# Dealing the blocks of U ahead unevenly over the three tiles of gates

## The chip, the cores and the metric

The kernel runs on one core of one Trainium2 chip. The metric is the device time of one launch in microseconds (us). Five engines run their own instruction queues in order: TensorE (PE, with PEld for its weight loads), VectorE (DVE), ScalarE (ACT), GpSimd (POOL) and SyncE (SP, which issues most DMAs). A plan made when the kernel is built fixes the order of every queue; on the chip an instruction waits only for the semaphores that it names.

## The reference

One decoder layer over 512 tokens of width 1024, all in float32. First comes token mixing (two attention groups, an output projection, a residual). Then comes a feed-forward part that looks experts up by product keys, and the change lies there:

```python
def chunk(hc):                                   # per token
    s1, s2 = scores of 8 heads against two sets of 128 keys
    v1, i1 = lax.top_k(s1, 16); v2, i2 = lax.top_k(s2, 16)
    best_s, best_pos = lax.top_k(16 x 16 sums, 16)
    expert = i1 * 128 + i2 at best_pos           # 8 x 16 of 16384 experts
    g = softmax(best_s)
    act = gelu(hc . u[expert])
    return sum over (head, k) of g * act * v[expert]
```

A last RMS norm follows.

## The kernel before

The 512 tokens are four tiles of 128. For tiles 0 to 2 the feed-forward part is dense: all 16384 experts are computed as 128 blocks of 128 experts, and a matrix of gates, nonzero at the chosen experts only, picks them. For tile 3 the 128 chosen rows of U and V per token are gathered by indirect DMA instead (`gather_ops`, L916).

**A block of U** (`u_block`, L874) loads 512 KB (SP), splits it into a high part (`uhi`, ScalarE) and a low part (`ulo`, VectorE, or GpSimd for every fourth block below 56), runs 24 matmuls (`p_u`, TensorE) and a Gelu (`a`, ScalarE). `raw`, `hi` and `lo` have two buffers each. The loads and splits have high priority in the plan (`UPRI`).

**The gates.** `route` (L713) scores the keys and takes the top 16 on VectorE, `choose` (L749) finds the experts, `spread` (L792) turns the result by TensorE transposes (`tp_s`) and makes three tables on VectorE (`o16`, `o8`). Then, for each tile, eight groups of sixteen tokens follow, each in two halves: `hot` (L816) makes one-hot factors on VectorE (`oh0` to `oh2`, two buffers each), `gates` (L831) multiplies them on TensorE (`p_g`, 16 matmuls a half), ScalarE copies the result out of PSUM (`st`, two copies a half), and after both halves SP stores 1 MB (`g_d`).

**The gathers of tile 3.** `gu` is a row of U gathered by GpSimd and multiplied on VectorE (L921). Its buffers are those of the four transposed queries `qT`, four of them, which come free as `route` has read them.

**U ahead.** The blocks of V need the gates of all three tiles, the blocks of U don't. So 56 blocks of U (`NAHEAD`) are dealt out among the work on the gates by `u_ahead`: `U0` of them ahead of the first tile's gates (L939, L941), then `GPAT[tg]` after each group of sixteen tokens (L959), then what is left (L962). The first 16 results (`NSPILL`) go out to DRAM (`a_d`). The planner then moves instructions by priority and buffers, so that what a queue holds is not quite the order of the code.

**The V part** (from L1042) has, for each of 128 blocks: a load of V (`v`), its split (`vhi`, `vlo`), a load of the spilled activations (`ar`) for the first 16, a load of the gates for every eighth (`gt`), the weights (`w`, `wh`, `wl`) and 18 matmuls (`acc`). From block 16 on a block of U follows each block of V.

Of the kernel before, what the change touches and what calls it, by code (L numbers as in the profile page):

```python
# [47 lines left out]
NGP = (0, 0, 0, 0, 1, 2, 3, 3)  # L48
M5 = 2
RLAG = 1  # L50
U0 = (4, 2)
GPAT = (2, 2, 2, 2, 2, 2, 2, 2)
WAN = (1, 2)
XAT = (0, 1)
UPRI = 1000
# [19 lines left out]
def hybrid_layer(ctx: ExitStack, tc, x, pos, wada, wada_n, cols, w_small, w_in_a, w_in_b, wuk, wuv,  # L75
# [15 lines left out]
    def one(name, tag="tp"):  # L91
        return ps.tile([P, 512], F32, tag=tag, name=name, bufs=BANKS[tag])
# [699 lines left out]
    def spread(j, sel3):  # L792

        i1 = rp.tile([P, 3, P], I32, tag="i1", name=f"i1_{j}")
        nc.vector.tensor_copy(i1[:, 0], sel3[:, 0])
        nc.vector.tensor_scalar(i1[:, 1], i1[:, 0], 4, None, op0=ALU.arith_shift_right)
        nc.vector.tensor_scalar(i1[:, 2], i1[:, 0], 15, None, op0=ALU.bitwise_and)
        f1 = rp.tile([P, 2, P], F32, tag="f1", name=f"f1_{j}")
        nc.vector.tensor_copy(f1, i1[:, 1:3])
        tp = one(f"tp_s{j}")  # L800
        for i, src in enumerate((f1[:, 0], f1[:, 1], sel3[:, 1], sel3[:, 2])):
            nc.tensor.transpose(tp[:, i * P:(i + 1) * P], src, ident)
        tt = rp.tile([P, 5, P], F16, tag="tt", name=f"tt{j}")
        nc.scalar.activation(tt[:, 0:3], tp[:, 0:3 * P].rearrange("p (i t) -> p i t", t=P), AF.Copy)
        nc.scalar.activation(tt[:, 3], tp[:, 3 * P:4 * P], AF.Copy, scale=GSCALE)
        nc.vector.scalar_tensor_tensor(tt[:, 4], tp[:, 3 * P:4 * P], GSCALE, tt[:, 3], op0=ALU.mult, op1=ALU.subtract)
        pairs = lambda i, n: tt[:, i].rearrange("p (q e) -> p q e", e=2).unsqueeze(2).to_broadcast([P, P // 2, n, 2])
        o16 = rq.tile([P, P // 2, 16, 2], F16, tag="o16", name=f"o16_{j}")
        o8 = [rq.tile([P, P // 2, 8, 2], F16, tag=f"o8_{i}", name=f"o8_{i}_{j}") for i in range(2)]
        nc.vector.tensor_tensor(o16, pairs(1, 16), iota8.unsqueeze(1).to_broadcast([P, P // 2, 16, 2]), op=ALU.is_equal)  # L810
        nc.vector.tensor_tensor(o8[1], pairs(0, 8), iota8[:, 0:8].unsqueeze(1).to_broadcast([P, P // 2, 8, 2]), op=ALU.is_equal)
        nc.vector.tensor_tensor(o8[0], o8[1], pairs(3, 8), op=ALU.mult)
        nc.vector.tensor_tensor(o8[1], o8[1], pairs(4, 8), op=ALU.mult)
        return tt, o16, o8

    def hot(j, tg, half, tt, o16, o8):  # L816

        sh, sh5 = [P, 4, NK, 2], [P, 4, 8, 16, 2]
        t0 = tg * 16 + half * 8
        qs = slice(t0 // 2, t0 // 2 + 4)  # L820
        oh = [rq.tile([P, 4, NK, 2], F16, tag=f"oh{i}", name=f"oh{i}_{j}_{tg}_{half}", bufs=2) for i in range(3)]
        nc.vector.tensor_tensor(oh[2], tt[:, 2, t0:t0 + 8].rearrange("p (q e) -> p q e", e=2).unsqueeze(2).to_broadcast(sh),
                                iota2.unsqueeze(1).to_broadcast(sh), op=ALU.is_equal)
        for i in range(2):
            nc.vector.tensor_tensor(oh[i].rearrange("p q (a b) e -> p q a b e", b=16), o8[i][:, qs].unsqueeze(3).to_broadcast(sh5),  # L825
                                    o16[:, qs].unsqueeze(2).to_broadcast(sh5), op=ALU.mult)
        return oh
# [46 lines left out]
    def u_block(b, psum):  # L874
        with tc.high_priority(offset=UPRI):
            raw = up.tile([P, KC, P], F32, tag="raw", name=f"u{b}", bufs=2)
            nc.sync.dma_start(raw.rearrange("p k e -> p (k e)"), ut[b])
            hi = up.tile([P, KC, P], F32R, tag="hi", name=f"uhi{b}", bufs=2)
            lo = up.tile([P, KC, P], F32R, tag="lo", name=f"ulo{b}", bufs=2)
            nc.scalar.activation(hi, raw, AF.Copy)  # L880
            (nc.gpsimd if b in UPOOL else nc.vector).tensor_tensor(lo, raw, hi.bitcast(F32), op=ALU.subtract)  # L881
        o = psum(f"p_u{b}")[:, :DT]
        for k in range(KC):
            mm3(o, hi[:, k], lo[:, k], h2[0][:, k], h2[1][:, k], k == 0, k == KC - 1)
        spilt = b < NSPILL
        a = up.tile([P, DT], F32, tag="as" if spilt else "a", name=f"a{b}", bufs=2 if spilt else NACT)
        nc.scalar.activation(a, o, AF.Gelu)  # L887
        if spilt:
            nc.sync.dma_start(a_d[b], a)
            a = a_d[b]  # L890
        acts.append(a)
# [3 lines left out]
    def u_ahead(n):  # L895
        for _ in range(n):
            if nu[0] < NAHEAD:
                u_block(nu[0], lambda n: one(n, ("pj", "po", "ix")[nu[0] % 3]))
                nu[0] += 1

    def chosen(j):
        sel3 = choose(j, *lists[j])
        if j == NT - 1:
            nc.vector.scalar_tensor_tensor(e0, sel3[:, 0], float(NK), sel3[:, 1], op0=ALU.mult, op1=ALU.add)
            nc.vector.tensor_copy(g0, sel3[:, 2])
        return sel3
# [31 lines left out]
    route(1, 0, *lists[0])  # L938
    u_ahead(U0[0])  # L939
    sel3 = chosen(0)  # L940
    u_ahead(U0[1])  # L941
    waiting = []

    def gates_all():
        while waiting:
            gates(*waiting.pop(0))

    for j, coming in ((0, (3, 1)), (1, (2,)), (2, ())):
        tt = spread(j, sel3)
        for tg in range(P // 16):  # L950
            for half in range(2):
                waiting.append((j, tg, half, hot(j, tg, half, *tt)))
            gates_all()
            for i, jn in enumerate(coming):
                if tg == WHEN[i][0]:
                    route(1, jn, *lists[jn])
                if tg == WHEN[i][1]:
                    sel3 = chosen(jn)
            u_ahead(GPAT[tg])  # L959
            for _ in range(NGP[tg] if j == ND - 1 else 0):  # L960
                next(gen)
    u_ahead(NAHEAD)  # L962
# [167 lines left out]
```

## Time and profile before

| what | us |
|---|---|
| median of 3 runs | 1616.62 (1614.98 to 1617.26) |
| the profiled execution | 1614.71 |
| its span | 1612.8 |

The profile's span is cut into stretches by hand, at marks on TensorE: the first matmul of U (441.3), the first matmul of the gates of tile 0 (497.5), of tile 1 (603.5), of tile 2 (688.5), the last of tile 2 (758.7), and the first matmul of V (781.2). After that the V part runs to the end of the span.

### The profile page before, as it was taken

How to read it: one execution, taken by the hardware profiler on the slowest of the kernel's cores; microseconds unless marked ns; L12 is line 12 of the kernel's file. 1: busy time of each engine (PE TensorE's matmuls, PEld its weight loads, DVE VectorE, ACT ScalarE, POOL GpSimd, SP SyncE). 2: the span in 40 equal slices, each digit the busy share in tenths (PEclk: the TensorE clock that was granted, in tenths of full speed). 3: DMA queues.
4: the chain of work that ended last, by engine and by line, in shares of the span. 5: the costliest groups of instructions: out<-in, count | busy, mean ns of one | idle time of the engine just before them, and what ended most of it. 6: DMA issues, size and time to landing. Idle time of an engine off the chain costs nothing.

```text
span 1612.8 us, 22930 instructions
## 1 busy us (share of the span) xinstructions
PE 1509.9 (94%) x8136; PEld 1328.4 (82%) x8138; DVE 1287.0 (80%) x2659; ACT 713.4 (44%) x1142; POOL 529.3 (33%) x403
## 2 busy tenths in 40 slices
PE   5887998999899989989999999999999999999997
PEld 5755776877688888889889999999999999988886
DVE  7899964856999999983569887878888788768886
ACT  4654544544245675765333333333333333323333
POOL 2333022212110220221016454554555445534420
PEclk7998997999999999999999999999999999999999
DMA  8643012514044654575979998999989999879974
GB/s 340 217 148 131 1 40 78 171 54 133 14 139 161 222 207 169 215 266 190 314 259 342 364 344 327 354 311 350 336 310 356 311 349 345 311 271 326 317 257 157
DMA packets 152899, 383.39 MB, mean 238 GB/s; under 512 B 11712, under 2 KB 66384, under 8 KB 149456
## 3 DMA queue, kind: packets, MB, share of 16 engines
q1 hardware_dynamic: 114912, 246.45, 45.0%
q0 software_dynamic: 36864, 134.23, 22.0%
q8 instruction: 64, 1.05, 0.3%
q10 hardware_dynamic: 1008, 1.24, 0.2%
q14 instruction: 51, 0.42, 0.1%
HBM read 349.36 MB, written 32.51 MB: 237 GB/s over the span
## 4 chain that ended last, share of the span: by engine, by line
PE 52%; DVE 3%; DMA 2%; issue 1%; ACT 1%; SPq 0%; POOL 0%; DVEq 0%; POOLq 0%; ACTq 0%
PE acc L1014 30%; PE p_u L149 7%; PE p_u L148 7%; PE p_u L147 7%; DMA ar<-a_d 1%; DVE gu L921 1%; DMA u<-in_ut_dram 1%; PE p_g L841 0%; DVE oh L825 0%; ACT st L844 0%; DVE vlo L993 0%; DMA x1b<-x_d 0%; DVE ulo L881 0%; DMA v<-in_pv_dram 0%; DVE o L1035 0%
## 5 line engine op out<-in xcount | busy, mean ns | idle before, releaser
L147 PE MATMUL p_u<-h,uhi 128*128 128x384 f32 x1024 | 349.7, 342 | 1.4 <-ACT a L887 1.4
L149 PE MATMUL p_u<-h,ulo 128*128 128x384 f32 x1024 | 349.2, 341 | 0.6 <-DVE ulo L881 0.5
L148 PE MATMUL p_u<-h,uhi 128*128 128x384 f32 x1024 | 348.8, 341 | 0.0
L913 POOL DMA_INDIRECT gu<-in_un_dram,e x128 | 191.5, 1496 | 296.6 <-DVE gu L921 201.5
L880 ACT ACTIVATE uhi<-u 128x1024 fp32r<-128x1024 f32 x128 | 135.8, 1062 | 292.2 <-PE p_u L148 250.9
L913 POOL DMA_INDIRECT gv<-in_pv_dram,e x128 | 191.2, 1493 | 208.6 <-DVE acc L932 163.2
L1014 PE MATMUL acc<-vhi,wh 128*128 128x512 f32 x768 | 237.1, 389 | 1.2 <-ACT wh L1006 1.2
L1014 PE MATMUL acc<-vlo,wh 128*128 128x512 f32 x768 | 237.4, 389 | 0.3 <-DVE vlo L993 0.3
L1014 PE MATMUL acc<-vhi,wl 128*128 128x512 f32 x768 | 237.1, 389 | 0.0
L1006 ACT ACTIVATE wh<-w 128x384 fp32r<-128x384 f32 x128 | 67.3, 526 | 303.4 <-issue 182.1
L147 PEld LDWEIGHTS p_u<-h,uhi 128*128 128x128 f32 x1024 | 195.0, 190 | 4.6 <-ACT a L887 1.7
L148 PEld LDWEIGHTS p_u<-h,uhi 128*128 128x128 f32 x1024 | 195.5, 191 | 2.9
L149 PEld LDWEIGHTS p_u<-h,ulo 128*128 128x128 f32 x1024 | 195.4, 191 | 1.6 <-DVE ulo L881 0.8
L1007 DVE TENSOR_TENSOR wl<-w,wh 128x384 fp32r<-128x384 f32 x128 | 71.5, 558 | 138.1 <-ACT wh L1006 137.8
L881 DVE TENSOR_TENSOR ulo<-u,uhi 128x1024 fp32r<-128x1024 f32 x114 | 139.0, 1219 | 51.9 <-ACT uhi L880 35.1
L1014 PEld LDWEIGHTS acc<-vlo,wh 128*128 128x128 f32 x768 | 144.0, 188 | 30.8 <-DVE vlo L993 1.0
L1014 PEld LDWEIGHTS acc<-vhi,wl 128*128 128x128 f32 x768 | 144.1, 188 | 30.2
L932 DVE SCALAR_TENSOR_TENSOR acc<-gv,w,acc 128x1024 f32<-128x1024 f32 x127 | 162.5, 1279 | 4.6 <-DMA gv<-in_pv_dram,e 4.6
L921 DVE SCALAR_TENSOR_TENSOR gu<-gu,h2n 128x1024 f32<-128x1024 f32 x128 | 158.8, 1255 | 8.0 <-DMA gu<-in_un_dram,e 7.7
L1014 PEld LDWEIGHTS acc<-vhi,wh 128*128 128x128 f32 x768 | 143.2, 188 | 26.0 <-ACT wh L1006 1.5
L993 DVE TENSOR_TENSOR vlo<-v,vhi 128x1024 fp32r<-128x1024 f32 x128 | 156.2, 1220 | 3.8 <-ACT vhi L992 3.8
L992 ACT ACTIVATE vhi<-v 128x1024 fp32r<-128x1024 f32 x128 | 135.6, 1059 | 9.2 <-PE acc L1014 4.3
(354 smaller groups left out, 2361.2 us busy)
## 6 DMA issues: line engine op xcount, KB each, us to landing
u<-in_ut_dram SPq DMA_DIRECT2D x128, 512.0 KB, 5.2
v<-in_pv_dram SPq DMA_DIRECT2D x128, 512.0 KB, 5.0
g_d<-st SPq DMA_DIRECT2D x24, 1024.0 KB, 4.8
gt<-g_d SPq DMA_DIRECT2D x48, 512.0 KB, 8.3
wada<-in_wada_dram SPq DMA_DIRECT2D x12, 1024.0 KB, 5.0
raw_b<-in_w_in_b_dram SPq DMA_DIRECT2D x12, 512.0 KB, 3.6
x<-in_x_dram SPq DMA_DIRECT2D x8, 512.0 KB, 4.5
raw_o<-in_w_out_dram SPq DMA_DIRECT2D x8, 512.0 KB, 3.5
```

What stands on the lines that cost most here:

```text
L147: nc.tensor.matmul(o, ahi, bhi, start=start, stop=False, **kw)
L148: nc.tensor.matmul(o, ahi, blo, start=False, stop=False, **kw)
L149: nc.tensor.matmul(o, alo, bhi, start=False, stop=stop, **kw)
L880: nc.scalar.activation(hi, raw, AF.Copy)
L881: (nc.gpsimd if b in UPOOL else nc.vector).tensor_tensor(lo, raw, hi.bitcast(F32), op=ALU.subtract)
L913: nc.gpsimd.indirect_dma_start(out=t, out_offset=None, in_=src, in_offset=bass.IndirectOffsetOnAxis(ap=e0[:, s:s + 1], axis=0))
L921: nc.vector.scalar_tensor_tensor(t, t, 1.0, h2n, op0=ALU.mult, op1=ALU.mult, accum_out=dot0[:, s:s + 1])
L932: nc.vector.scalar_tensor_tensor(acc0, t, w0[:, s:s + 1], acc0, op0=ALU.mult, op1=ALU.add)
L992: nc.scalar.activation(hi, raw, AF.Copy)
L993: nc.vector.tensor_tensor(lo, raw, hi.bitcast(F32), op=ALU.subtract)
L1007: last[0] = nc.vector.tensor_tensor(wl, w, wh.bitcast(F32), op=ALU.subtract).ins
L1014: nc.tensor.matmul(accs[2 * j + n], l[:, js], r[:, n * 512:(n + 1) * 512], start=b == 0 and i == 0, stop=b == NK - 1 and i == 2)
```

## The change

Three constants and one index change. `U0` has ten blocks ahead of the first tile's gates in place of six. `GPAT` has a row for each tile: three blocks after every group of tile 0, two in tile 1, one after every second group in tile 2, in place of two throughout. Both come to 54 blocks, and L962 adds two.

```diff
-U0 = (4, 2)
-GPAT = (2, 2, 2, 2, 2, 2, 2, 2)
+U0 = (6, 4)
+GPAT = ((3,) * 8, (2,) * 8, (1, 0) * 4)
...
     for j, coming in ((0, (3, 1)), (1, (2,)), (2, ())):
         tt = spread(j, sel3)
         for tg in range(P // 16):
...
-            u_ahead(GPAT[tg])
+            u_ahead(GPAT[j][tg])
```

No instruction's work changes; the plan orders them anew on every queue. Counted in the order of the queues:

| at this point of TensorE's queue | matmuls of U ahead of it, before | now |
|---|---|---|
| first gates of tile 0 | 262 | 273 |
| first gates of tile 1 | 681 | 849 |
| first gates of tile 2 | 991 | 1243 |
| last half of the gates of tile 2 | 1250 | 1331 |
| first matmul of V | 1363 | 1392 |

| on VectorE | before | now |
|---|---|---|
| between the first one-hots of tile 0 and those of tile 1: `ulo` | 12 | 18 |
| the same stretch: `gu` | 2 | 9 |
| from there to the first one-hots of tile 2: `ulo` | 11 | 12 |
| the same stretch: `gu` | 4 | 0 |

**End of tile 0, GpSimd's queue.** `gu` are gathers, `ulo` the splits of a block of U, `idx` a cast of `route`. Before:

```order
L913 DMA gu3_7867<-in_un_dram,e0_3429 128x1024
L881 TENSOR_TENSOR ulo28_6453<-u28_6450,uhi28_6452 128x1024
L913 DMA gu4_7870<-in_un_dram,e0_3429 128x1024
L913 DMA gu5_7873<-in_un_dram,e0_3429 128x1024
L733 CAST idx2_3511<-iu1_2_5941 128x16x4
L881 TENSOR_TENSOR ulo32_6693<-u32_6690,uhi32_6692 128x1024
```

And now:

```order
L913 DMA gu3_7933<-in_un_dram,e0_3429 128x1024
L881 TENSOR_TENSOR ulo28_6011<-u28_6008,uhi28_6010 128x1024
L913 DMA gu4_7936<-in_un_dram,e0_3429 128x1024
L913 DMA gu5_7939<-in_un_dram,e0_3429 128x1024
L913 DMA gu6_7996<-in_un_dram,e0_3429 128x1024
L913 DMA gu7_7999<-in_un_dram,e0_3429 128x1024
L913 DMA gu8_8002<-in_un_dram,e0_3429 128x1024
L913 DMA gu9_8250<-in_un_dram,e0_3429 128x1024
L881 TENSOR_TENSOR ulo32_6197<-u32_6194,uhi32_6196 128x1024
```

Four more gathers stand ahead of the split of block 32.

**The same place, VectorE's queue**, from the last one-hots of tile 0 (`oh1_0_7_1`) to the tables of tile 1 (`tt1`, `o16_1`, `o8_1`; `eq`, `sel3`, `i1` and `f1` belong to `choose` and `spread`). Before:

```order
L825 TENSOR_TENSOR oh1_0_7_1_5751<-o8_1_0_4587,o16_0_4585 128x1024
...
L921 SCALAR_TENSOR_TENSOR gu0_7618,dot0_3431<-gu0_7618,h2n_3426 128x1024
L782 TENSOR_TENSOR sel3_1_5511<-eq1_1_1_5545 128x64
L921 SCALAR_TENSOR_TENSOR gu1_7741,dot0_3431<-gu1_7741,h2n_3426 128x1024
L810 TENSOR_TENSOR o16_1_5879<-tt1_5875,iota8_95 128x2048
L806 SCALAR_TENSOR_TENSOR tt1_5875<-tp_s1_5870,tt1_5875 128x128
```

And now:

```order
L825 TENSOR_TENSOR oh1_0_7_1_6114<-o8_1_0_4723,o16_0_4721 128x1024
L921 SCALAR_TENSOR_TENSOR gu3_7933,dot0_3431<-gu3_7933,h2n_3426 128x1024
L921 SCALAR_TENSOR_TENSOR gu4_7936,dot0_3431<-gu4_7936,h2n_3426 128x1024
L921 SCALAR_TENSOR_TENSOR gu5_7939,dot0_3431<-gu5_7939,h2n_3426 128x1024
L881 TENSOR_TENSOR ulo31_6164<-u31_6161,uhi31_6163 128x1024
L921 SCALAR_TENSOR_TENSOR gu6_7996,dot0_3431<-gu6_7996,h2n_3426 128x1024
L921 SCALAR_TENSOR_TENSOR gu7_7999,dot0_3431<-gu7_7999,h2n_3426 128x1024
L921 SCALAR_TENSOR_TENSOR gu8_8002,dot0_3431<-gu8_8002,h2n_3426 128x1024
L881 TENSOR_TENSOR ulo33_6230<-u33_6227,uhi33_6229 128x1024
L881 TENSOR_TENSOR ulo34_6426<-u34_6423,uhi34_6425 128x1024
L881 TENSOR_TENSOR ulo35_6459<-u35_6456,uhi35_6458 128x1024
L806 SCALAR_TENSOR_TENSOR tt1_6271<-tp_s1_6266,tt1_6271 128x128
```

Six gathers and four splits now stand between the two.

**End of tile 2, SP's queue**, from the last store of gates. Before:

```order
L847 DMA g_d2_85<-st2_7_7888 128x2048
L877 DMA u56_8649<-in_ut_dram 128x1024
L980 DMA gt0_8086<-g_d0_83 128x8x128
L980 DMA gt0_8086<-g_d1_84 128x8x128
L877 DMA u57_8721<-in_ut_dram 128x1024
L980 DMA gt0_8086<-g_d2_85 128x8x128
L984 DMA v0_8090<-in_pv_dram 128x1024
L877 DMA u58_8793<-in_ut_dram 128x1024
L998 DMA ar0_8097<-a_d0_67 128x384
L984 DMA v1_8122<-in_pv_dram 128x1024
```

And now:

```order
L847 DMA g_d2_85<-st2_7_7954 128x2048
L877 DMA u59_8862<-in_ut_dram 128x1024
L980 DMA gt0_8086<-g_d0_83 128x8x128
L980 DMA gt0_8086<-g_d1_84 128x8x128
L980 DMA gt0_8086<-g_d2_85 128x8x128
L877 DMA u60_8934<-in_ut_dram 128x1024
L984 DMA v0_8090<-in_pv_dram 128x1024
L998 DMA ar0_8097<-a_d0_67 128x384
L877 DMA u61_9006<-in_ut_dram 128x1024
L984 DMA v1_8122<-in_pv_dram 128x1024
```

The load of V's first block now stands behind `u60`, which waits until VectorE has split block 58; it stood behind `u57`, which waited for block 55.

## Rows read from the trace of the kernel before

**Rows 1.** The page, parts 1 and 4: busy times, chain by engine.

```profile
PE 1509.9 (94%) x8136; PEld 1328.4 (82%) x8138; DVE 1287.0 (80%) x2659; ACT 713.4 (44%) x1142; POOL 529.3 (33%) x403
PE 52%; DVE 3%; DMA 2%; issue 1%; ACT 1%; SPq 0%; POOL 0%; DVEq 0%; POOLq 0%; ACTq 0%
```

**Rows 2.** Busy time by stretch: PE, PEld, DVE, ACT, POOL; clock, DMA, GB/s.

```profile
441.30:497.50 56.20, 51.94 (x280) 50.44 (x278) 53.34 (x233) 23.20 (x30) 6.33 (x6) 0.95 0.44 138
498.60:602.10 103.50, 94.19 (x672) 88.64 (x671) 101.02 (x345) 67.89 (x83) 23.70 (x15) 0.98 0.59 204
603.50:688.50 85.00, 76.11 (x573) 71.75 (x572) 79.29 (x216) 55.02 (x66) 14.42 (x9) 0.94 0.56 199
688.50:758.70 70.20, 64.94 (x516) 61.94 (x517) 43.63 (x60) 43.24 (x53) 12.70 (x6) 0.95 0.63 224
758.70:781.20 22.50, 19.95 (x114) 19.32 (x113) 6.64 (x7) 9.37 (x14) 0.00 (x0) 1.00 0.87 298
870.00:1500.00 630.00, 630.00 (x3163) 571.46 (x3162) 510.79 (x643) 224.16 (x308) 316.70 (x214) 1.00 0.92 331
```

**Rows 3.** TensorE's waits from 441 to 760: total, times, longest.

```profile
PE p_g L841 <- DVE oh L825: 16.0, 12, 3.1
PE p_g L841 <- ACT st L844: 4.4, 5, 2.4
PE tp_s L802 <- DVE sel L782: 3.8, 1, 3.8
PE p_sc L720 <- DVE tt L806: 3.0, 1, 3.0
```

**Rows 4.** TensorE in order of time: start, length, instruction [idle before it].

```profile
451.64 0.33 PE L149 MATMUL p_u<-h,ulo 128*128 128x384 f32 x1
...
452.16 0.33 PE L149 MATMUL p_u<-h,ulo 128*128 128x384 f32 x1
...
603.53 1.09 PE L841 MATMUL p_g<-oh,oh 128*128 128x128 f16 x16
...
625.59 1.89 PE L841 MATMUL p_g<-oh,oh 128*128 128x128 f16 x16 [3.10 <-DVE oh L825]
...
758.07 0.62 PE L841 MATMUL p_g<-oh,oh 128*128 128x128 f16 x8 [0.51 <-ACT st L844]
...
781.17 0.74 PE L1014 MATMUL acc<-vhi,wh 128*128 128x512 f32 x2 [1.19 <-ACT wh L1006]
```

**Rows 5.** VectorE in order of time, at two places.

```profile
487.21 0.29 DVE L729 MAX8 v<-wk 128x8 f32<-128x128 f32 x1
...
677.78 1.22 DVE L921 SCALAR_TENSOR_TENSOR gu<-gu,h2n 128x1024 f32<-128x1024 f32 x1
...
678.93 3.40 DVE L921 SCALAR_TENSOR_TENSOR gu<-gu,h2n 128x1024 f32<-128x1024 f32 x1
...
684.20 1.21 DVE L881 TENSOR_TENSOR ulo<-u,uhi 128x1024 fp32r<-128x1024 f32 x1
685.34 0.68 DVE L812 TENSOR_TENSOR o<-o,tt 128x1024 f16<-128x1024 f16 x1
```

**Rows 6.** GpSimd in order of time, at the second of them.

```profile
678.51 2.74 POOL L881 TENSOR_TENSOR ulo<-u,uhi 128x1024 fp32r<-128x1024 f32 x1
```

**Rows 7.** The gathers' line L913, 540 to 890: issue in ns; landing in us.

```profile
L913 POOL DMA_INDIRECT gu<-in_un_dram,e x32: 932/1677/1982, 545.4 to 880.2; - x32
...
DMA to landing us min/median/max: 5.0/6.6/11.5
```

**Rows 8.** ScalarE in order of time, a group of tile 2.

```profile
744.63 1.06 ACT L880 ACTIVATE uhi<-u 128x1024 fp32r<-128x1024 f32 x1 [2.67 <-PE p_u L148]
...
745.96 3.80 ACT L844 ACTIVATE st<-p_g 128x512 f32<-128x512 f32 x4
```

**Rows 9.** SP's queue in order of time, end of tile 2.

```profile
768.95 0.69 SPq L877 DMA_DIRECT2D u<-in_ut_dram  x1
...
770.31 1.51 SPq L984 DMA_DIRECT2D v<-in_pv_dram  x1
```

## The prediction

> **What bounds the kernel now.** I read the page's busy times and chain first, then the busy time by stretch, the waits of TensorE, and the timelines at the joints of the stretches. TensorE is busy for 94% of the span and holds 52% of the chain that ended last; no other engine holds over 3% [rows 1]. In the V part it is busy for 630 of 630 us [rows 2], so a matmul taken out of that part, or an earlier start of it, shortens the kernel by as much. What can be won lies ahead of it, between 441 and 781. There TensorE waited 27.2 us, of which 16.0 in front of gate matmuls for one-hots of VectorE, 4.4 for ScalarE's copies, 3.8 and 3.0 in front of the transposes and the scoring [rows 3]. After a long wait it also runs at the lower of its two clock levels, 1.2 in place of 2.4 GHz: the sixteen gate matmuls behind the wait of 3.10 took 1.89 us, others 1.09 [rows 4], and the mean granted clock of that tile is 0.94 [rows 2].
>
> VectorE is the one that is late: in tile 0 it is busy for 101.0 of 103.5 us and in tile 1 for 79.3 of 85.0, in tile 2 only for 43.6 of 70.2 [rows 2]. The blocks of U are TensorE's filler while VectorE works on routing. A U matmul follows the last after 0.173 us (three in 0.52) [rows 4]; that is 4.16 us a block, and sixteen gate matmuls take 1.0 to 1.1.
>
> **The change part by part.** All sums are against the profiled execution: 1614.71 us, 1.9 below the median of the runs.
>
> The ten blocks ahead of tile 0 bring little: 262 U matmuls already stood ahead of the first gates, now 273. I take the start of tile 0 as unmoved on VectorE.
>
> *Tile 0, from 498.6, by VectorE's sum.* To its 101.0 us of work [rows 2] come six more splits, 1.14 each from start to start, 6.9; seven more gathered rows, 1.15 each, 8.1; five routing operations that used to run during the wait at the transposes, 0.29 each, 1.5 [rows 5]. GpSimd splits one block more beside it: a gathered row during such a split took 3.40 in place of 1.22 [rows 5, 6], so 2.2. Then waits that the new order brings at the end of the tile. The gather `gu6` takes the buffer of `gu3`; it lands 6.6 after its issue [rows 7], and VectorE has two rows and one split, 3.4, to do meanwhile: a wait of 3.3 with 0.1 for the semaphore. Behind `gu6` GpSimd must issue `gu9` (1.7 [rows 7]) before it splits block 32 (2.7 [rows 6]); TensorE then runs the other 22 matmuls of block 32 (3.8) and block 33 (4.2); ScalarE and VectorE split block 35 (1.1 [rows 8] and 1.1) before the tables of tile 1. That is 14.6, in which VectorE has two rows and three splits, 5.7: a wait of 8.9. Waits 12.2, sum 131.9, so VectorE has its first one-hots of tile 1 at 630.5, against 602.1, and TensorE starts on them 1.4 later, at 631.9, against 603.5. It has 168 more U matmuls behind it by then, 29.1 us, for 28.4 us more time: 0.7 won.
>
> *Tile 1.* 394 U matmuls in place of 310, 68.3 us, sixteen halves of gates at 1.0, and 1.7 for transposes and scoring: 86.0. Its first group stays short of filler: before, gates to gates took 22.1 [rows 4]; now 96 U matmuls in place of 97 stand there, and one split more, so the wait of 3.10 grows to 4.5, with 2.0 for the low clock (three long waits cost that tile 6% of 85 us, 5.1, or 1.7 each [rows 2]). I keep 2 us for the second lump, choosing. Together 94.5 in place of 85.0, so tile 2 starts at 726.4. 84 matmuls, 14.6 us, for 9.5: 5.1 won.
>
> *Tile 2.* TensorE has 88 U matmuls (15.2) and 16.0 of gates, 31; VectorE about 31 (43.6 less six splits, three rows and a held one); ScalarE 32 copies at 0.95 and four times a split and a Gelu at 1.33 between start and next copy [rows 8], 35.7. ScalarE sets it, and TensorE's last gates are out some 1.2 ahead: 34.5 in place of 70.2. They end at 760.9, against 758.7 [rows 4], with 81 more U matmuls done (14.1).
>
> *The end, where the filler is gone.* Behind the last gates before stood 113 U matmuls, 19.6 us, which covered most of the 22.5 us until V could start [rows 2]. Now 61 stand there, 10.6. V's first block was loaded 11.6 after the last gates, behind `u57` [rows 9]. Now it stands behind `u60`, which waits for block 56: 37 matmuls (6.4), split (1.1 and 1.1), two issues (0.8), 9.4. From that load to V's first matmul were 10.9 [rows 4, 9]; I take 10.4, as `ar0` stands better. So 19.8 after 760.9: 780.7, against 781.2. TensorE idles 9 us, costing 2.0 of low clock; and 29 matmuls that V's part held are done, 5.0.
>
> Sum: −0.5 + 2.0 − 5.0 = −3.5 us. Some 12 us are won ahead of the last gates and 8 given back behind them. 1614.7 − 3.5 = 1611.2 for a profiled run, 1613.1 by the median.
>
> Bounds: a gather lands in 5.0 to 11.5 [rows 7], −1.6 to +4.9. A split on GpSimd holds VectorE for nothing or for 2.2; up to five fall in tiles 0 and 1 with two groups of three on the path, −2.2 to +6.6. V's first matmul comes 16 (the load landing in 5 and its split) to 22.5 after the last gates, −3.8 to +2.7.
>
> The Trainium skill, "GPSIMD Engine Reference", section "8. Key points", says that GpSimd shares its SBUF interfaces with VectorE and that the two contend when a VectorE instruction has two SBUF inputs. The trace agrees in the row of 3.40. By that rule the three of the twelve moved splits that are GpSimd's leave a tile where VectorE idles for tiles where it does not, and nearly every operation there has two SBUF inputs; that is the mechanism of the slower rival below.
>
> **The rivals.**
>
> *The gathers and block 32 cost nothing.* If TensorE rather than VectorE is late at the end of tile 0, the gathers land in time and block 32 is split before it is wanted. The 12.2 go: −15.7, median 1600.9. For it: TensorE has three blocks a group in tile 0, 12.5 and 2.1 us, and the last groups have no routing. Against: VectorE had 2.5 us to spare in 103.5 [rows 2] and gets 17 more.
>
> *VectorE is held more often (slower).* Each group of routing or choosing ends in gates for which TensorE waits; three splits of GpSimd that fall on these at 2.2, and a gather of 11.5 at `gu6`, make 11.5: +8.0, median 1624.6. It decides from some 6 us of them on. For it: waits for VectorE are already the largest [rows 3], and VectorE's queue has the gathers in front of splits that TensorE needs at once. Against: some operations between are short or have one input.
>
> *V's start is not tied to the filler.* If V's first matmul comes 22.5 after the last gates as before, 2.7 are lost: −0.8, median 1615.8. For it: the load stands behind a split block in both plans, and landing varies.
>
> **How the numbers follow.** 0.2% is 3.2 us, about what a measurement of this kernel can tell from no change. The forecast with its own range (−8 to +1) gets 0.37: 0.18 faster, 0.18 the same, 0.01 slower. The first rival gets 0.20, all faster. The second gets 0.26, all slower. The third gets 0.17: 0.04 faster, 0.10 the same, 0.03 slower. So faster 0.42, the same 0.28, slower 0.30. The range reaches from the first rival to the second, 1602 to 1625, since they hold nearly half of the chance.
>
> **What would show it.** In the profile of the changed kernel: first gates of tile 1 near 632 and of tile 2 near 726, last gates near 761; TensorE waiting for a split of GpSimd (block 32) at some 615; VectorE waiting for a gather once in tile 0; V's first matmul near 781 after the longest wait of TensorE, 9 us, for V's load or split; ScalarE without a gap in tile 2. The forecast is wrong if the last gates end before 750 or after 770, or if V's first matmul follows them by less than 14 us.

## The result and the profile after

The changed kernel takes 1622.29 us (median of 15 runs, 1618.55 to 1626.67) beside 1614.22 of the kernel before on the same chip: ratio 1.0053, 95% interval 1.0042 to 1.0064. It is slower by half a percent, 8.1 us by the medians, where 1613.1 and a gain of 3.5 were forecast. The profiled execution's span is 1620.5 us, against 1612.8.

The page of the changed kernel, parts 1 and 4, against [rows 1]: busy time of each engine, and the chain that ended last.

```profile
PE 1515.0 (93%) x8136; PEld 1332.7 (82%) x8138; DVE 1285.5 (79%) x2659; ACT 713.5 (44%) x1142; POOL 539.0 (33%) x403
PE 57%; DVE 14%; issue 10%; DMA 3%; ACT 3%; POOL 1%; DVEq 0%; POOLq 0%; ACTq 0%; SPq 0%
```

The two chains can't be set side by side: the one before is followed back to 666 us only, the one now to 178, so that its 14% of VectorE (3% before) hold 490 us of work that the other leaves out. Where time was lost, the stretches tell. Busy time by stretch of the changed kernel, cut at the same marks on TensorE as [rows 2]: PE, PEld, DVE, ACT, POOL, then granted clock, DMA share, GB/s. (Tile 0 is cut at TensorE's first gates here, at VectorE's mark in [rows 2].)

```profile
442.90:497.60 54.70, 52.47 (x291) 51.03 (x289) 52.65 (x225) 24.53 (x32) 6.69 (x7) 0.98 0.48 151
497.60:640.40 142.80, 128.90 (x854) 123.82 (x854) 121.14 (x383) 78.16 (x96) 38.75 (x24) 0.94 0.60 204
640.40:737.50 97.10, 87.81 (x656) 83.94 (x656) 76.19 (x206) 59.21 (x72) 18.44 (x7) 0.98 0.50 175
737.50:773.50 36.00, 33.79 (x345) 30.08 (x346) 31.46 (x48) 33.49 (x39) 0.00 (x0) 0.95 0.69 264
773.50:791.50 18.00, 10.96 (x62) 10.31 (x61) 4.80 (x5) 6.81 (x8) 0.00 (x0) 0.96 0.92 310
860.00:1500.00 640.00, 639.45 (x3209) 579.68 (x3208) 522.32 (x663) 227.23 (x312) 331.00 (x222) 1.00 0.93 333
```

The V part is as full as before. Tile 0 is the stretch to look at: VectorE is busy for 121.1 of 142.8 us and TensorE for 128.9, so neither is full, and the clock fell to 0.94. What TensorE waited for from 442 to 792 (total, times, longest), against [rows 3]:

```profile
PE p_g L841 <- DVE oh L825: 14.6, 8, 3.8
PE p_g L841 <- ACT st L844: 5.9, 8, 2.3
PE acc L1014 <- ACT wh L1006: 5.7, 1, 5.7
...
PE p_sc L720 <- DVE tt L806: 2.7, 1, 2.7
```

The 3.8 at the transposes is gone, and the wait in front of V's first matmul grew from 1.19 [rows 4] to 5.7. The three others add up to 23.2 beside 23.4 in [rows 3], though 157 more U matmuls stand in tile 0 to fill them. New, too, are 4.1 in front of U matmuls whose split was late (0.5 before).

To compare kernels whose blocks lie differently I use TensorE's lost time: the length of a stretch less its U matmuls at 0.1735 us and less 1.5, 17.7, 17.7, 16.0 and 0 for gates and scoring. It holds what TensorE waited and what a low clock cost it. "V part" is what follows V's first matmul, as if 1363 U matmuls stood ahead of it, as before.

| stretch: lost time, us | before, two profiles | changed |
|---|---|---|
| U ahead of tile 0's gates | 9.2, 9.7 | 5.8 |
| tile 0 | 15.6, 17.3 | 25.2 |
| tile 1 | 13.5, 12.1 | 11.0 |
| tile 2 | 9.3, 7.0 | 4.7 |
| last gates to V | 2.9, 1.7 | 7.4 |
| V part | 831.6, 833.5 | 834.0 |
| sum, from the first U matmul on | 882.1, 881.3 | 888.1 |

Three stretches gained 8.9 us together against the mean of the two; tile 0 lost 8.8, the end 5.1, the V part 1.5: 6.4 in sum.

### The profile page after: what moved, and what is told of

It reads as the page before. It is cut to its first block, busy times and chain, and to the rows that moved or that the text cites. A ratio compares the mean times of both kernels' runs of the same rounds, so it can differ in the third digit from the quotient of the medians.

```text
span 1620.5 us, 22934 instructions
## 1 busy us (share of the span) xinstructions
PE 1515.0 (93%) x8136; PEld 1332.7 (82%) x8138; DVE 1285.5 (79%) x2659; ACT 713.5 (44%) x1142; POOL 539.0 (33%) x403
## 4 chain that ended last, share of the span: by engine, by line
PE 57%; DVE 14%; issue 10%; DMA 3%; ACT 3%; POOL 1%; DVEq 0%; POOLq 0%; ACTq 0%; SPq 0%
PE acc L1014 26%; PE p_u L147 7%; PE p_u L148 7%; PE p_u L149 7%; DVE ulo L881 2%; PE po L560 1%; DMA u<-in_ut_dram 1%; DVE oh L825 1%; PE p_g L841 1%; DMA gu<-in_un_dram,e 1%; DVE iu L730 1%; PE pl L534 1%; DVE wk L728 1%; PE tp L550 1%; DVE iu L731 1%
## 5 line engine op out<-in xcount | busy, mean ns | idle before, releaser
L913 POOL DMA_INDIRECT gu<-in_un_dram,e x128 | 190.3, 1487 | 298.8 <-DVE gu L921 242.0
L913 POOL DMA_INDIRECT gv<-in_pv_dram,e x128 | 193.6, 1512 | 203.1 <-DVE acc L932 154.3
L921 DVE SCALAR_TENSOR_TENSOR gu<-gu,h2n 128x1024 f32<-128x1024 f32 x128 | 154.6, 1222 | 18.1 <-DMA gu<-in_un_dram,e 17.7
L992 ACT ACTIVATE vhi<-v 128x1024 fp32r<-128x1024 f32 x128 | 135.6, 1059 | 12.2 <-PE acc L1014 6.7
```

What stands on the lines that cost most here:

```text
L913: nc.gpsimd.indirect_dma_start(out=t, out_offset=None, in_=src, in_offset=bass.IndirectOffsetOnAxis(ap=e0[:, s:s + 1], axis=0))
L921: nc.vector.scalar_tensor_tensor(t, t, 1.0, h2n, op0=ALU.mult, op1=ALU.mult, accum_out=dot0[:, s:s + 1])
```

## The experiments

Where no other is named, the edit is to the changed kernel; all compute the whole reference. Ratios are to the kernel before, timed on the same chip.

**Only the front.** Is work at the front harmless?

```diff
-GPAT = ((3,) * 8, (2,) * 8, (1, 0) * 4)
+GPAT = ((2,) * 8, (2,) * 8, (2, 1) * 4)
```

> Ten blocks ahead of tile 0's gates as in the changed kernel, but tiles 0 and 1 keep two blocks a group; the four blocks come out of tile 2 (two and one by turns). 118 U matmuls stand behind the last gates (before 113, changed kernel 61), and tile 0 holds 2 gathered rows of U as before. Theory A (the changed kernel loses in tile 0, where three blocks a group tie VectorE's queue to the split buffers, the gathers and TensorE, and at the end, where the filler behind the last gates is gone): neither loss is here, so 1610 to 1615, no slower than before, V's first matmul some 22 us after the last gates. Rival B (work moved to the front costs by itself, since the stretch up to tile 0's gates grew by 1.6 us in the changed kernel): 1616 to 1618, and first gates of tile 0 later than 498.5 again.

1621.18, ratio 1.0051 (1.0036 to 1.0067): a miss for both. The loss sat in tile 1 (95.4 us, 19.2 lost). Its timeline, all engines in order of time (start, length, instruction, idle before it and what ended that):

```profile
668.04 13.32 SPq L877 DMA_DIRECT2D u<-in_ut_dram  x2
...
670.98 10.03 POOL L881 TENSOR_TENSOR ulo<-u,uhi 128x1024 fp32r<-128x1024 f32 x1 [21.46 <-ACT uhi L880]
...
681.45 0.86 SPq L847 DMA_DIRECT2D g_d<-st  x2
...
687.86 3.64 ACT L844 ACTIVATE st<-p_g 128x512 f32<-128x512 f32 x4 [8.82 <-DMA g_d<-st]
...
688.94 1.01 PE L841 MATMUL p_g<-oh,oh 128*128 128x128 f16 x8 [9.41 <-ACT st L844]
```

GpSimd's split of block 40, 2.35 to 2.9 us in most places, took 10.03 beside a row of one-hots on VectorE. Until it was done, at 681.0, the buffer `raw` was not free, so SP was held in its next two loads of U for 13.32; the stores of gates stood behind them, ScalarE's copies waited for the stores, TensorE for the copies.

**That split and another like it moved to VectorE.** Block 24's had taken 7.73.

```diff
-UPOOL = tuple(range(0, 56, 4))
+UPOOL = tuple(b for b in range(0, 56, 4) if b not in (24, 40))
```

> The run with only the front changed (ten blocks ahead of tile 0, two a group in tiles 0 and 1, the four taken from tile 2), with the splits of blocks 24 and 40 on VectorE instead of GpSimd. In that run these two took 7.73 and 10.03 us on GpSimd beside a row of one-hots on VectorE (others 2.35 to 2.6), and behind the second SP's queue, the stores of the gates, ScalarE's copies and TensorE (9.41 idle) stood still. Theory L (the front by itself costs nothing; the loss is the slow split and what queues behind it): tile 1 shortens from 95.4 to 84 to 88, the wait of 9.41 is gone, and the time is 1609 to 1614 beside 1613.8 of the kernel before, the same or up to 0.3% faster. Rival M (the four blocks at the front cost by the plan around them, whatever engine splits): 1618 to 1622, with another wait of that size.

1613.33, ratio 0.9990 (0.9975 to 1.0006), tile 1 87.4, the wait gone: L, not M. The slow split in tile 1 had cost 8 us. The 7.73 in tile 0 had cost little: that tile took 112.0 with it and 111.1 without, so what a slow split costs depends on its place.

**Only tile 0.**

```diff
-U0 = (6, 4)
-GPAT = ((3,) * 8, (2,) * 8, (1, 0) * 4)
+U0 = (4, 2)
+GPAT = ((3,) * 8, (2,) * 8, (1,) * 8)
```

> Three blocks a group in tile 0, two in tile 1, one in tile 2, and six blocks ahead of tile 0's gates as before; 118 U matmuls stand behind the last gates, so that the end keeps its filler. Theory A (losses in tile 0 and at the end): tile 0 is as poor as in the changed kernel (TensorE's lost time in it 18 to 22 us in place of 12), V's first matmul comes some 22 us after the last gates with TensorE idle for 3, and the 4.5 of the end and the 2.4 behind it are back: 1614 to 1618. Rival C (the end alone costs; tile 0's loss is only what the later tiles would have lost): 1609 to 1613. Rival D (tile 0 is the whole of it): 1620 to 1623.

1621.80, ratio 1.0058 (1.0042 to 1.0074). The time is D's. The end lost 4.1 only, with 118 U matmuls as filler (3 by A); tile 0 lost 23.8, more than A had. No split of GpSimd in this tile 0 took over 2.91, and VectorE waited only 1.5 for high parts; it was busy for 117.0 of 127.4 us and waited 8.8 for four gathers, all at the tile's end. So three blocks a group lose as much here with no slow split.

**No gathers ahead.**

```diff
-NGP = (0, 0, 0, 0, 1, 2, 3, 3)
+NGP = (0,) * 8
```

> The changed kernel with no gathered row of U among the tiles' gates: all 128 come beside the V part. Tile 0 then has 18 splits and no gathered row on VectorE (changed kernel 18 and 9), and SP's loads of U don't wait for splits behind gathers. Theory E (the gathers that the new plan pulled into tile 0 are what spoils it: 9 rows at 1.15 and 7.2 us of waits for their landing): tile 0 shortens from 142.8 to 127 to 133 and the time falls to 1609 to 1615. Rival A (three blocks a group wait for their own split buffers, which TensorE, ScalarE and VectorE free one by one): tile 0 stays over 137 and the time within 3 of the changed kernel, 1619 to 1624.

1619.71, ratio 1.0043 (1.0027 to 1.0059); tile 0 139.9. The gathers in tile 0 are not the cause (E falls). VectorE had nine rows less, and instead stood 26.8 us at splits that waited for their high part.

**Three buffers for a block of U**, first in the changed kernel, then in the kernel before.

```diff
-NACT = 40
-NSPILL = 16
+NACT = 32
+NSPILL = 24
...
-            raw = up.tile([P, KC, P], F32, tag="raw", name=f"u{b}", bufs=2)
+            raw = up.tile([P, KC, P], F32, tag="raw", name=f"u{b}", bufs=3)
```

and the same for `hi` and `lo` and wherever else these buffers are named.

> The changed kernel with three buffers in place of two for a block of U (raw, hi, lo), paid for by spilling eight more blocks of activations (24 in place of 16). Theory K (with 18 splits in tile 0 VectorE's queue and TensorE's are tied through two buffers: VectorE stands at a split that waits for ScalarE, which waits for TensorE to free a buffer, and the one-hots behind it come late): VectorE's waits for the high parts in tile 0 fall from 12.2 to under 6, tile 0 shortens from 142.8 to 130 to 136, and the time against the kernel before with the same three buffers is 0 to +4. Rival G (VectorE's own work and GpSimd's splits beside it set the tile): tile 0 stays over 139 and the difference stays at +6 to +10.

> The kernel before with the same three buffers and 24 spilled blocks: the control for the run above. Theory K: VectorE bounds tile 0 there by its own work (101 of 103.5 busy with two buffers), so a third buffer brings tile 0 under 2 us; 1610 to 1617, within 0.3% of the kernel before, with eight more loads of activations in the V part. If it gains as much in tile 0 as the changed kernel does, the two buffers bind both plans alike and don't explain the difference.

1619.89 (ratio 1.0035, 1.0022 to 1.0048) against 1618.45 (1.0022, 1.0012 to 1.0033): 1.4 us apart instead of 8. That is not the buffers' worth: the total of the kernel before came out above K's range, since one split on GpSimd now took 11.36 in tile 1 there and TensorE stood 11.25 behind it (18.5 lost in that tile, in place of 13.5 and 12.1). The buffers did nothing for its tile 0 (108.4 us). In the changed kernel tile 0 went to 135.5. VectorE's waits in tile 0 (total, times, longest), first of the changed kernel with two buffers:

```profile
DVE ulo L881 <- ACT uhi L880: 12.2, 8, 4.4
DVE gu L921 <- DMA gu<-in_un_dram,e: 7.2, 2, 5.1
```

and with three:

```profile
DVE gu L921 <- DMA gu<-in_un_dram,e: 10.0, 4, 3.8
DVE ulo L881 <- ACT uhi L880: 2.3, 3, 1.7
```

The waits of splits for their high part fell from 12.2 to 2.3, as K had it; by tile 0 G falls, by the time it is not tested. Nor is the buffers' part shown by itself: in this run GpSimd's split of block 20, 4.35 in the changed kernel's tile 0, took 2.55, and the runs below bring the tile to the same length by that split alone.

**Three buffers and no gathers ahead.** The edits of the two, so to the one with three buffers:

```diff
-NGP = (0, 0, 0, 0, 1, 2, 3, 3)
+NGP = (0,) * 8
```

> The changed kernel with three buffers for a block of U (24 spilled blocks) and no gathered row of U among the gates, so that VectorE's 10.0 us of waits for gathers and nine rows of 1.15 leave tile 0. Theory K with the gathers as the second cause: tile 0 goes from 135.5 to 122 to 128, and the time from 1619.9 to 1612 to 1617, less what the nine rows cost in the V part (1 to 2 in the run without gathers and two buffers). Rival O (with the buffers loosened TensorE's own 117.6 of tile 0 and ScalarE's copies bind, not the gathers): tile 0 stays over 131, the time 1618 to 1621.

1617.20 (1.0015, 0.9998 to 1.0032); tile 0 132.3: O by the tile, between the two by the time. The 10.0 of waits for gathers and the nine rows were worth 3.2 to the tile, and the V part grew by 4.8 with the rows that it now holds.

**Two splits of the changed kernel moved to VectorE, then one of them, then four.** GpSimd's split of block 20 took 4.35 in tile 0, that of block 44 7.39 in tile 1.

```diff
-UPOOL = tuple(range(0, 56, 4))
+UPOOL = tuple(b for b in range(0, 56, 4) if b not in (20, 44))
```

> The changed kernel with the splits of blocks 20 and 44 on VectorE instead of GpSimd, which took 4.35 and 7.39 there beside one-hots. Theory K (the two buffers between the splits and TensorE make tile 0's loss): TensorE's wait of 1.9 for the split of block 44 goes and little else; 1618 to 1622 and tile 0 still 139 to 144. Rival N (slow GpSimd splits are the changed kernel's loss as well): 1610 to 1616, tile 0 under 136.

1615.32 (1.0012, 0.9992 to 1.0031); tile 0 135.5: N, against my K, which had allowed little. For block 20 alone:

```diff
-UPOOL = tuple(range(0, 56, 4))
+UPOOL = tuple(b for b in range(0, 56, 4) if b not in (20,))
```

> The changed kernel with the split of block 20 alone on VectorE instead of GpSimd (4.35 us there, begun beside one-hots in tile 0). Theory N (the slow split holds block 20's buffer, so that SP loads block 22 late, ScalarE waits for it and VectorE's one-hots stand behind the split): with blocks 20 and 44 moved tile 0 took 135.5 in place of 142.8; with 20 alone tile 0 is 134 to 137 again, tile 1 keeps its 97, and the time is 1616 to 1619. Rival P (the gain of those two was tile 1's and a chance of the order): tile 0 stays over 139, the time 1619 to 1622.

1618.32 (1.0033, 1.0019 to 1.0046); tile 0 135.4, tile 1 98.4: N. One split of GpSimd held tile 0 for 4.3 to 7.4 us, since the profiles that have it took 142.8, 142.2 and 139.7 (the last two from runs below that change the end alone). The way it did is in the changed kernel's timeline, all engines:

```profile
542.17 4.35 POOL L881 TENSOR_TENSOR ulo<-u,uhi 128x1024 fp32r<-128x1024 f32 x1 [23.11 <-ACT uhi L880]
...
544.40 2.21 DVE L782 TENSOR_TENSOR sel<-eq 128x64 f32<-128x64 f16 x1
...
552.51 1.20 DVE L881 TENSOR_TENSOR ulo<-u,uhi 128x1024 fp32r<-128x1024 f32 x1
...
553.74 14.44 SPq L877 DMA_DIRECT2D u<-in_ut_dram  x4
...
561.17 1.06 ACT L880 ACTIVATE uhi<-u 128x1024 fp32r<-128x1024 f32 x1 [5.99 <-DMA u<-in_ut_dram]
...
562.26 1.23 DVE L881 TENSOR_TENSOR ulo<-u,uhi 128x1024 fp32r<-128x1024 f32 x1 [1.41 <-ACT uhi L880]
...
569.37 0.93 PE L841 MATMUL p_g<-oh,oh 128*128 128x128 f16 x7 [3.79 <-DVE oh L825]
```

and in that of the kernel with block 20 on VectorE:

```profile
551.05 15.04 SPq L877 DMA_DIRECT2D u<-in_ut_dram  x4
...
557.81 1.06 ACT L880 ACTIVATE uhi<-u 128x1024 fp32r<-128x1024 f32 x1 [3.51 <-DVE v L727]
...
561.78 1.10 PE L841 MATMUL p_g<-oh,oh 128*128 128x128 f16 x16 [0.63 <-DVE oh L825]
...
567.55 1.13 PE L841 MATMUL p_g<-oh,oh 128*128 128x128 f16 x16 [1.32 <-DVE oh L825]
```

The slow split also held VectorE (a `sel` of 2.21 in place of 0.21). The next split of VectorE came late, with it the free buffer, SP's load (553.74 in place of 551.05), ScalarE's high part (561.17 in place of 557.81), the split behind it, and the one-hots: TensorE waited 3.79 in place of 0.63 and 1.32. Another wait, 2.30 for ScalarE's copies at 598.7, went too. The granted clock took the larger share: tile 0 of the same kernel reads

```profile
498.20:633.60 135.40, 123.78 (x853) 118.48 (x852) 120.80 (x384) 78.15 (x96) 37.19 (x23) 0.99 0.61 215
```

so TensorE was busy 5.1 us less for the same matmuls, at 0.99 in place of 0.94, and idle 2.3 less. In stretches of 4 us at the changed kernel's waits of 2.93, 3.79, 2.30 and 2.68 the granted clock read down to 0.65, 0.50, 0.74 and 0.57 (0.5 is 1.2 GHz, 1.0 is 2.4).

With four moved:

```diff
-UPOOL = tuple(range(0, 56, 4))
+UPOOL = tuple(b for b in range(0, 56, 4) if b not in (20, 28, 44, 52))
```

> The changed kernel with the splits of blocks 20, 28, 44 and 52 on VectorE: with 20 and 44 moved, blocks 28 and 52 took 6.47 and 5.56 on GpSimd. Theory N: TensorE's waits of 1.6 and less for GpSimd go and tile 0 comes to 132 to 136, 1612 to 1616, level with the kernel before, since V's start still loses 5. Rival R (VectorE, 119.5 busy in tile 0, can't take more splits): tile 0 137 to 141 and 1617 to 1621.

1617.84 (1.0024, 1.0012 to 1.0036), tile 0 138.2: R's ranges, though not its reason. VectorE was busy for 120.5 us, no more than with two moved (119.5); but TensorE waited 4.8 for one of its splits near the end of tile 0, and the end lost 10.9.

**The control: the kernel before with blocks 20 and 44 moved.** To the kernel before:

```diff
-UPOOL = tuple(range(0, 56, 4))
+UPOOL = tuple(b for b in range(0, 56, 4) if b not in (20, 44))
```

> The kernel before with the splits of blocks 20 and 44 on VectorE, the control for the changed kernel with the same two moved (1615.3). In the kernel before no split among the gates takes over 3.27 us on GpSimd, so there is no slow one to take away. Theory N: nothing is gained, two splits more of 1.2 on a VectorE that is busy for 101 of 103.5 us in tile 0 cost 1 to 4; 1613 to 1618. Rival Q (moving two splits helps any plan): 1606 to 1610, the same 7 us as in the changed kernel, and the explanation falls.

1609.09, ratio 0.9965 (0.9952 to 0.9979): Q's range, and by what was written ahead of the run N falls as the explanation of the difference. No split among this kernel's gates had been slow, and yet moving two won 0.35%, beside 0.41% in the changed kernel. Its tile 0 took 106.3 us, beside 106.0 and 107.7, with 13 more U matmuls in it; by lost time tile 0 won 2.8, tile 1 2.6 and tile 2 2.0. Why is not shown. With the same two moved the dealing still costs 0.47% (1.0012 against 0.9965), beside 0.53% with none. By lost time that difference is 6.0 at the end, 3.5 in the V part and 4.3 in tile 0 (8.8 with no split moved), less 4.9 gained elsewhere.

**The end: V's loads first.** The load of `v0` to `v2` raised in the plan:

```diff
-        nc.sync.dma_start(raw, pv[b * P:(b + 1) * P, :])
+        with tc.high_priority(offset=UPRI) if b < VRB else nullcontext():
+            nc.sync.dma_start(raw, pv[b * P:(b + 1) * P, :])
```

> The changed kernel with the loads of the first blocks of V raised in the plan, so that on SP v0, v1 and v2 stand right behind the load of block 59 of U instead of behind the gates' loads and block 60's. Theory A (V's first matmul is late since its load stands behind a load that waits for a block of U): v0's load is issued some 6 us earlier (778.5 in place of 784.3), V's first matmul comes 12 to 14 us after the last gates in place of 18.0, and the time falls by 3 to 6, to 1616 to 1619. Rival F (the gates' loads and the weights made from them bound V's start): V's first matmul stays at 17 to 18 us after the last gates, and the time stays at 1621 to 1623.

1625.68 (1.0083, 1.0066 to 1.0100), V's first matmul 23.7 after the last gates: a miss for both. V was split early, but `ar0` was now the late load. With the loads of the gates, `v0` and `ar0` all raised, for the first block only (the same line ahead of `v0`'s load and of the three loads of the gates):

```diff
-            nc.sync.dma_start(a, acts[b])
+            with tc.high_priority(offset=UPRI) if b == 0 else nullcontext():
+                nc.sync.dma_start(a, acts[b])
```

> The changed kernel with all five loads that V's first matmul needs (three of the gates, v0 and the spilled activations ar0) raised in the plan, so that on SP they stand ahead of the load of block 60 of U, which waits for a block of U. With v0 alone raised, ar0 was issued 2.5 us later and V's first matmul came 23.7 after the last gates. Theory A (the order behind the last gates is the end's loss): ar0 is issued some 3 to 5 us earlier than in the changed kernel, V's first matmul comes 12 to 15 after the last gates in place of 18.0, and the time is 1616 to 1620. Rival J (the transfers themselves, with the DMA engines 0.92 to 0.94 busy in that stretch, are late whatever their order): 17 to 20 after the last gates and 1620 to 1624.

1621.01 (1.0046, 1.0030 to 1.0061), V's first matmul 17.3 after the last gates: J. In the changed kernel the end reads (SP's issues, then ScalarE and TensorE)

```profile
775.20 0.32 SPq L847 DMA_DIRECT2D g_d<-st  x1
778.06 0.33 SPq L877 DMA_DIRECT2D u<-in_ut_dram  x1
778.49 3.06 SPq L980 DMA_DIRECT2D gt<-g_d  x3
783.85 0.34 SPq L877 DMA_DIRECT2D u<-in_ut_dram  x1
784.25 0.42 SPq L984 DMA_DIRECT2D v<-in_pv_dram  x1
784.72 0.42 SPq L998 DMA_DIRECT2D ar<-a_d  x1
...
789.85 1.06 ACT L992 ACTIVATE vhi<-v 128x1024 fp32r<-128x1024 f32 x1 [3.13 <-DMA v<-in_pv_dram]
...
791.55 0.79 PE L1014 MATMUL acc<-vhi,wh 128*128 128x512 f32 x1 [5.75 <-ACT wh L1006]
```

and with the five loads first

```profile
780.13 1.95 SPq L986 DMA_DIRECT2D v<-in_pv_dram  x1
782.14 0.42 SPq L1001 DMA_DIRECT2D ar<-a_d  x1
...
788.01 0.56 DVE L1002 TENSOR_TENSOR w<-ar,gt 128x384 f32<-128x384 f32 x1 [1.72 <-DMA ar<-a_d]
...
789.18 1.22 PE L1017 MATMUL acc<-vhi,wh 128*128 128x512 f32 x2 [5.06 <-ACT wh L1009]
```

The issue of `ar0` moved up by 0.9 against the last gates (10.3 behind them in place of 11.2), V's first matmul by 0.7. Order buys little; what helps is filler. The versions with 118 U matmuls behind the last gates lost 3.5 to 4.4 there, those with 55 to 61 lost 6.8 to 10.9 (13.1 with `v0` raised alone). That the transfers themselves set the 17 us, with the DMA engines 0.92 busy, is argued, not shown.

**The start.** The kernel before once more, with no edit:

> The kernel before, once more, for a second profile of it. The profiles so far differ by up to 3.9 us at the first matmul of U (441.1 to 445.0), though what runs ahead of it is the same work in the same order, and the shift is there within the first 100 us. Theory H (run variation): the ratio to the runs of before is 1.000 within 0.002, and the first matmul of U comes anywhere in 441 to 445. Rival I (the changed plan moves the start): 441.3 within 0.3 again.

1613.07 (0.9988, 0.9975 to 1.0001). Its first matmul of U in the profile:

```profile
446.62 0.88 PE L147 MATMUL p_u<-h,uhi 128*128 128x384 f32 x1
```

beside 441.3 in the first profile of it. H, if a little beyond its range: the start varies by 5 us, and the changed kernel's 442.9 says nothing of the plan. All sums above begin at that matmul.

**A faster version.** The version with only the front changed, with four splits moved:

```diff
-UPOOL = tuple(range(0, 56, 4))
+UPOOL = tuple(b for b in range(0, 56, 4) if b not in (24, 28, 40, 44))
```

> The run with only the front changed, with the splits of blocks 24, 28, 40 and 44 on VectorE: with 24 and 40 moved (1613.3), blocks 28 and 44 took 4.85 and 5.57. Theory N: another 1 to 4 us, 1609 to 1613, the first version faster than the kernel before by some 0.1 to 0.2%. Rival R (VectorE, nearly full in tiles 0 and 1, pays 1.2 for each split moved): 1613 to 1618.

1606.22 (0.9954, 0.9936 to 0.9971): faster than N's range. Is that the dealing? The control, the kernel before with that edit of `UPOOL` alone, beside a repeat:

> The kernel before with the splits of blocks 24, 28, 40 and 44 on VectorE: the same four as in the version with ten blocks ahead of tile 0 and the four blocks taken from tile 2, which took 1606.2. Theory S (the gain of that version is the splits', not the dealing's; moving blocks 20 and 44 gave the kernel before 0.35% already): 1604 to 1609, level with that version within 0.15%. Rival T (ten blocks ahead help once no split is slow, by the 3 us or so of TensorE's lost time ahead of tile 0's gates and as much in tile 2): 1609 to 1613, 3 to 6 us slower than that version.

> The version with ten blocks ahead of tile 0, two a group in tiles 0 and 1, four fewer in tile 2 and the splits of blocks 24, 28, 40 and 44 on VectorE, once more beside its control on one chip: 1604 to 1609, ratio to the kernel before 0.994 to 0.997.

The kernel before with the four splits moved took 1602.67 (0.9932, 0.9907 to 0.9957), the repeat 1607.30 (0.9956, 0.9938 to 0.9974). S, and more than S: all of the gain is the splits', and the dealing is at best nothing. The kernel before with four splits moved is the fastest version that ran. Its tiles 0 and 1, in the columns of the table by stretch, with the clock at 1.00 and 0.98:

```profile
497.70:601.20 103.50, 97.40 (x711) 91.86 (x710) 101.25 (x350) 69.64 (x84) 16.64 (x12) 1.00 0.60 209
601.20:682.00 80.80, 74.74 (x579) 70.41 (x579) 77.52 (x217) 54.81 (x66) 11.58 (x8) 0.98 0.61 210
```

## Why the prediction was wrong, point by point

From the first matmul of U on, the forecast was −3.5 us and the profile shows +6.1. By the prediction's own sign it is wrong, since the last gates ended at 773.5, after 770. The 52% of the chain that it starts from are of a chain that reaches back to 666 us only; the waits and the busy times of the stretches, on which its sums rest, are read rightly. By the prediction's own steps:

- **The start.** "The ten blocks ahead of tile 0 bring little": TensorE's lost time there fell by 3.4, more than little. It counts into the start of tile 1 below, which is measured from the first matmul of U.
- **Tile 0, the step that failed.** "TensorE starts on them 1.4 later, at 631.9 ... 0.7 won." It was 640.4, less 1.6 of the start: 638.8, so 6.9 late. VectorE had its first one-hots of tile 1 at 637.45, forecast 630.5. Its work was 117.3 us up to there (119.7 forecast), its waits 21.7 (12.2 forecast). The waits at the end of the tile, behind its last one-hots at 606.9, came nearly as forecast in their sum:

```profile
614.29 1.23 DVE L921 SCALAR_TENSOR_TENSOR gu<-gu,h2n 128x1024 f32<-128x1024 f32 x1 [2.14 <-DMA gu<-in_un_dram,e]
...
620.58 1.23 DVE L921 SCALAR_TENSOR_TENSOR gu<-gu,h2n 128x1024 f32<-128x1024 f32 x1 [5.06 <-DMA gu<-in_un_dram,e]
...
626.34 1.23 DVE L881 TENSOR_TENSOR ulo<-u,uhi 128x1024 fp32r<-128x1024 f32 x1 [2.24 <-ACT uhi L880]
...
631.97 1.23 DVE L881 TENSOR_TENSOR ulo<-u,uhi 128x1024 fp32r<-128x1024 f32 x1 [4.40 <-ACT uhi L880]
```

  These are 13.8: 7.2 at gathers (3.3 forecast) and 6.6 at splits (8.9 forecast, by way of block 32 on TensorE; ScalarE stood for the loads of U instead, 3.39 and 4.19). What the sum put at nothing is the waits of VectorE ahead of that, 7.8, of which 5.5 at six splits whose high part was late. With 24 blocks in the tile, splits of VectorE, GpSimd and loads of SP take turns on two buffers, and block 20's slow split delayed those behind it. With that split moved, the waits ahead of the end are 1.8 and those at the end 12.8, and tile 1 starts at 632.3 on the same scale, against 631.9 forecast. In the changed kernel TensorE also took 2.9 in place of 1.4 from VectorE's one-hots to the gates, at a clock of 0.57 from 633 to 637, behind its wait of 2.68. The prediction priced such a split at 2.2 on VectorE, and gave it no price for the buffer that it holds or, in this tile, for the clock that falls behind the waits. That is the account of this one plan: the version with only tile 0 changed lost 23.8 there without a slow split, and moving splits won time in the kernel before as well.
- **Tile 1.** Forecast 94.5, measured 97.1: 2.6 more. A second slow split (block 44, 7.39) is in it; with both moved it took 93.4.
- **Tile 2.** Forecast 34.5, measured 36.0. ScalarE was the fullest engine beside TensorE, as forecast.
- **The end.** Forecast 19.8 from the last gates to V, measured 18.0; TensorE idle, forecast 9, lost 7.4. The mechanism held, though not the reason given for V's load: the order on SP hardly matters.
- **The V part.** 29 matmuls fewer were to save 5.0, less 2.0 of low clock: 3.0. It is shorter by 2.6.

The differences are 6.9 in tile 0, 2.6, 1.5, −1.8 and 0.4: 9.6 together. So "some 12 us are won ahead of the last gates and 8 given back behind them" came out as 0.9 won (13.2 us more for 81 matmuls of 0.1735) and 6.9 given back.

The slower rival had the time (1624.6 against 1622.3) and named two engines that had a part in it. That the time fits is partly luck: 1.6 of it is the start, which varies by itself. Its mechanism was half right: a split of GpSimd held tile 0, but through a buffer and the queues behind it, and the larger effect runs the other way: by the timelines it is VectorE's operations that slow GpSimd's split (4.35 to 10.03 in place of 2.4). The rival in which the gathers cost nothing is out (1600.9). That V's start is not tied to the filler is out too.

Three things stay open. Profiles of the changed kernel's tile 0 differ: 142.8, and 142.2 and 139.7 where only the end's loads were moved. Moving block 20's split won 0.20% by the timed ratios (1.0053 to 1.0033), but no run moved it alone in the kernel before, and by the control with two splits moved nearly all of that gain may be what any plan wins. And so most of the 0.53% is put on the end, the V part and tile 0 by profiles alone; no run brought the filler back to the changed kernel with its three tiles as they are.

## What to carry to other kernels

Where two engines are bound to each other through two buffers and both are nearly full, as in tile 0 here, the longer sum of work did not give the stretch: follow each buffer round its loop (load, split, matmul, free) and ask what one late turn stops. An engine that helps out on the side, as GpSimd does here, must be priced by what it holds, its buffer and the queues behind it, and not by its own time. And before a gain is put down to a change of order, run the same side edit on the kernel before: here that gave the fastest kernel of all.

## What the runs showed of the hardware

- GpSimd's split of 128x1024 takes 2.35 to 2.9 us in four places of five. The others took 3.0 to 11.4 us, those of 7.4 and more beside one-hots and other f16 operations of VectorE that ran back to back (0.68 each). Either engine can be the one that waits: in the version with only the front changed one split of 2.35 at 518.18 ran while a one-hot took 2.79, and in the changed kernel an operation of 0.21 took 2.21 at the end of the slow split. The Trainium skill, "GPSIMD Engine Reference", section "8. Key points", says that the two engines contend when a VectorE instruction has two SBUF inputs. The trace agrees (0.68 became 2.79, 2.4 became 10.03), and shows that GpSimd can be the one that loses most by it.
- Moving two or four of 14 such splits to a VectorE that was 98% busy in tile 0 made the kernel before faster by 0.35% and 0.68%.
- The time to the first matmul of U varies between executions of one kernel, 441.3 and 446.6 us, nearly as much as the effect under study.
